# The first norm of a two-layer trunk: q and k of both token halves in four banks, the order of four engines given by hand

## The chip, the cores and the metric

The kernel runs on one core of one Trainium2 chip. The metric is device microseconds from start to end of the program. A core has TensorE (PE, with its weight load PEld), VectorE (DVE), ScalarE (ACT), GpSimd (POOL) and SyncE (SP), which here only issues DMAs. Products are written to eight PSUM banks of 128 x 512 float32.

## The reference

x and the result are 1024 tokens x 1024 features, float32. Two layers, each a token mixer and a SwiGLU, with adaLN: c gives shift, scale and gate of every sub-layer. The change touches only the beginning of layer 0:

```
mod = silu(c) @ ada_w[0] + ada_b[0]          # 6 x 1024: sh1, sc1, g1, sh2, sc2, g2
h = rms_norm(x, norm1_g[0]) * (1 + sc1) + sh1
q, k, v, f_logit = split(h @ w_in)           # 1024, 1024, 1024, 16 columns
cum = cumsum(log_sigmoid(f_logit + b_f))     # over the tokens
# 16 heads of 64: softmax(q k^T / 8 + cum_t - cum_s, causal) @ v, then w_out
```

Behind it come the attention's output product, the SwiGLU of layer 0, layer 1 (gated linear attention and a second SwiGLU) and a last norm.

## The kernel before, in words

**Precision.** Every large product is done in three float32r passes: operands are split into hi and lo (`split`, L159 cast on ACT, L160 subtract on DVE; weights by `load_w`, L202 on ACT, L205 three quarters on POOL and one on DVE), and `mm3` (L237 to L239) multiplies hi by hi, hi by lo, lo by hi.

**The first norm.** Eight tiles of 128 tokens (`xt`) are loaded; `ss_half` squares four of them on ACT with a sum (L439), takes rstd (DVE L441, a power on POOL L442) and scales the tiles by it. The work then runs over eight blocks d of 128 features. For each d, `ada0_mod` sums the rows of the adaLN matrix for shift and scale: 128 rows k times cact in eight pieces, of which NPE[d] go to PE as small matmuls (L462) and 8 - NPE[d] to DVE (L468 the first, L470 the others); two matmuls per column with ones (L472) add up the partitions into `mp`; DVE writes `modc` (L473) and `amul` (L333). `h_block(d, hf)` transposes four tiles of a token half to features by tokens (L479), scales and shifts on ACT (y, L481), rounds hi on ACT (L483) and subtracts lo on DVE or POOL (L484). `first_k` multiplies the block into three banks: f (16 gate columns, L491 and L492), q and k of the first head pair. `first_v` does the same for the values of the first half's tokens in two more banks (L817 to L819). All blocks of the first half are done, `first_evac` empties the banks (q: L603 to L607, k: L613 to L620, gates: L219, L220 and L780 to L786, after the second half the logarithm, the running sum `cum` over tokens and its way through DRAM to the tiles `cum_s`, which the attention's scores need); then the second half goes through the same banks.

**Behind it.** `v_half(0, 1)` makes the values of the second half (L237 to L239, output vps). Then for seven head pairs p `weave` interleaves `attention(p)` with the q, k and v products of the next pair (qk_b, vps_b), in proportion to planned costs. The sums for the other four adaLN parts of layer 0 (`ada_steps`, L367 and L369 on DVE) are spread over the same time.

**Order.** The program is written in one order, and a scheduler then sets the order of each engine's instructions by a timeline of its own; data dependencies are kept by semaphores, and an engine runs its instructions in the order that stands. Buffers are rings: a tile takes over a slot when the slot's last reader is done. SP issues DMAs in order. A few orders are pinned by hand further on (`issue_after`, the lags of `weave`).

Of the kernel before, what the change touches and what calls it, by code (L numbers as in the profile page):

```python
# [9 lines left out]
F32 = mybir.dt.float32  # L10
# [43 lines left out]
def trunk(ctx, tc, x, c, ada_w, ada_b, norm1_g, norm2_g, ffn_w_in, ffn_w_out,  # L54
# [244 lines left out]
    load_x(2)  # L299
    load_x(3)  # L300
    load_ada0(0)
    bf = cst.tile([16, 1], F32, name="bf")
    nc.sync.dma_start(bf, fox_b_f.rearrange("o h -> h o"))
# [32 lines left out]
    def ada_steps(l, j, acc_of, raw_of, w):  # L336
# [11 lines left out]
        for c0 in range(0, D, w):  # L348
            acc = acc_of([P, w], F32, f"acc{l}{j}{c0}")
            for k in range(8):  # L350
                if w == D or c0 == k == 0:
                    load()
                raw = got.popleft()
                if w < D:
                    load()
                    yield ADA_A
                    if k == 0:
                        nc.scalar.mul(acc, raw, cact[:, 0:1])
                    else:
                        nc.scalar.mul(raw, raw, cact[:, k:k + 1])  # L360
                        nc.gpsimd.tensor_add(acc, acc, raw)  # L361
                    yield ADA_B
                    continue
                for q in range(0, w, 256):
                    cs = slice(q, q + 256)
                    if k == 0:
                        nc.vector.tensor_scalar(acc[:, cs], raw[:, cs], cact[:, 0:1], None, op0=ALU.mult)  # L367
# [68 lines left out]
    def ss_half(hf):  # L436
        for t in range(4 * hf, 4 * hf + 4):
            sq = sqr([P, D], BF16, f"sq{t}")
            nc.scalar.activation(sq, xt[t], AF.Square, accum_out=ssx[:, t:t + 1])  # L439
        cs = slice(4 * hf, 4 * hf + 4)  # L440
        nc.vector.tensor_scalar(rstd[:, cs], ssx[:, cs], 1.0 / D, EPS, op0=ALU.mult, op1=ALU.add)  # L441
        nc.gpsimd.tensor_tensor(rstd[:, cs], rstd[:, cs], mhalf[:, 0:4], op=ALU.pow)  # L442
        for t in range(4 * hf, 4 * hf + 4):
            r = rstd[:, t:t + 1]
            if hf == 0 and t % 2 == 0:
                nc.vector.tensor_scalar(xt[t], xt[t], r, None, op0=ALU.mult)
            elif hf == 0 and t == 1:
                nc.scalar.activation(xt[t], xt[t], AF.Copy, scale=r)
            else:
                nc.gpsimd.tensor_scalar(xt[t], xt[t], r, 1.0, op0=ALU.mult, op1=ALU.mult)  # L450

    VLAG, XD = 1, 4
    NPE = (4, 4, 4, 0, 0, 0, 0, 0)

    def ada0_mod(d):

        npe = NPE[d]
        mp = mp0([P, 2], F32, f"mp{d}")
        part = lambda k: araw[(d, k // 4)][:, k % 4]
        for j in range(2):  # L460
            for k in range(npe):
                nc.tensor.matmul(mp[:, j:j + 1], part(k)[:, j, :], cact[:, k:k + 1], start=k == 0 and j == 0,  # L462
                                 stop=k == 7 and j == 1)
        if npe < 8:
            acc = sm.tile([P, 2, P], F32, tag="t1k", name=f"acc0{d}")
        for k in range(npe, 8):
            if k == npe:
                nc.vector.tensor_scalar(acc, part(k), cact[:, k:k + 1], None, op0=ALU.mult)  # L468
            else:
                nc.vector.scalar_tensor_tensor(acc, part(k), cact[:, k:k + 1], acc, op0=ALU.mult, op1=ALU.add)  # L470
        for j in range(2 if npe < 8 else 0):
            nc.tensor.matmul(mp[:, j:j + 1], acc[:, j, :], ones, start=npe == 0, stop=npe == 0 or j == 1)  # L472
        nc.vector.tensor_add(modc[:, 0, 0:2, d], mp, vec[:, d:d + 16:8])  # L473
        make_a(0, 0, slice(d, d + 1))

    def h_block(d, hf):
        tp = tp0([P, HALF], F32, f"xp{d}{hf}")
        for i in range(4):
            nc.tensor.transpose(tp[:, psl(i)], xt[4 * hf + i][:, psl(d)], ident)  # L479
        y = yv()  # L480
        nc.scalar.activation(y, tp, AF.Identity, scale=acol(0, 0, d), bias=mcol(0, 0, d))  # L481
        hi, lo = hT[d].hi[:, hsl(hf)], hT[d].lo[:, hsl(hf)]
        nc.scalar.copy(hi, y)  # L483
        (nc.gpsimd if d % 2 == 1 else nc.vector).tensor_sub(lo, y, hi.bitcast(F32))  # L484

    def first_acc(hf):
        return [(w, par([P, HALF], F32, f"{nm}s{hf}")) for nm, w in (("f", wf), ("q", wq0), ("k", wk0))]

    def first_k(d, hf, acc):
        ps = acc[0][1]  # L490
        nc.tensor.matmul(ps, wf[:, d, :], hT[d].hi[:, hsl(hf)], start=d == 0, stop=False)  # L491
        nc.tensor.matmul(ps, wf[:, d, :], hT[d].lo[:, hsl(hf)], start=False, stop=d == 7)  # L492
        for w, ps in acc[1:]:
# [282 lines left out]
    def first_evac(hf, acc):
        cs = hsl(hf)
        f = zt[:, cs]
        sum16(f, ze[:, cs], acc[0][1])
        nc.scalar.activation(ze[:, cs], f, AF.Abs, bias=bf)  # L780
        nc.vector.tensor_scalar(zt[:, cs], f, bf, 0.0, op0=ALU.add, op1=ALU.min)
        nc.scalar.activation(ze[:, cs], ze[:, cs], AF.Exp, scale=-1.0)
        if hf:
            nc.scalar.activation(ze, ze, AF.Ln, bias=1.0)
            nc.vector.tensor_sub(zt, zt, ze)
            nc.vector.tensor_tensor_scan(cum, zt, zt, 0.0, ALU.add, ALU.bypass)  # L786
            nc.sync.dma_start(cum_d, cum)
            load_cum(0)
            load_cum(1)
        q_evac(acc[1][1], qkt[0], hf)  # L790
        k_evac(acc[2][1], qkt[0], hf)
# [14 lines left out]
    vts[0] = []  # L806
    ss_half(0)
    acc = first_acc(0)
    vacc = [par([P, 2, 256], F32, f"vps0{tp}") for tp in range(2)]

    def first_v(d):
        wv = wvs[0][d // 4]
        for tp in range(2):
            for i in range(2):
                ts_ = psl(2 * tp + i)
                p_, a_ = vacc[tp][:, i, :], (hT[d].hi[:, ts_], hT[d].lo[:, ts_])
                nc.tensor.matmul(p_, a_[0], wv.hi[:, d % 4, :], start=d == 0 and i == 0, stop=False)  # L817
                nc.tensor.matmul(p_, a_[0], wv.lo[:, d % 4, :], start=False, stop=False)
                nc.tensor.matmul(p_, a_[1], wv.hi[:, d % 4, :], start=False, stop=d == 7 and i == 1)  # L819

    def pre(d):
        ada0_mod(d)
        if d + 3 < 8:
            load_ada0(d + 3)
        h_block(d, 0)

    pre(0)
    for d in range(8):
        if d == 0:
            feed.depth = 1  # L830
            wvs[0] = [feed.next()]
        if d == 2:
            wvs[0].append(feed.next())
        if d < 7:
            pre(d + 1)
        first_k(d, 0, acc)
        if d >= VLAG:
            first_v(d - VLAG)
        if d == XD:
            for t in range(4, 8):  # L840
                load_x(t)
            ss_half(1)
    for d in range(8 - VLAG, 8):
        first_v(d)
    first_evac(0, acc)
    acc = first_acc(1)
    for tp in range(2):
        v_split(0, tp, vacc[tp])
    h_block(0, 1)
    for d in range(8):  # L850
        if d < 7:
            h_block(d + 1, 1)
        first_k(d, 1, acc)
    first_evac(1, acc)
# [1034 lines left out]
```

## Time and profile before

| | |
|---|---|
| runs, median of 3 | 2449.29 us (2447.56 to 2454.5) |
| span of the profiled execution | 2446.2 us |
| its own time | not on the page; the median above stands beside it |
| PE busy | 2385.6 us, 98% of the span |
| DVE, ACT, POOL busy | 1701.0, 1193.2, 1151.3 us |
| q, k and f of the second half ready on PE | 97 us |
| first score evacuated with cum | 116.2 us |

Rows of a timeline read: start in us, busy us of the merged group, engine, line, operation, output <- inputs, shapes, count; in brackets the engine's idle time before it and what ended it. Rows of the stretches read: the stretch, its length, busy us and instructions of PE, PEld, DVE, ACT and POOL, the granted PE clock, the DMA share and GB/s. A PE row's length holds the draining of the pipeline, so the distance of two starts is the time that a product costs.

### The profile page before, as it was taken

The page shows a single profiled execution, that of the slowest core. Times are in us where ns is not written, and L with a number is a line of the kernel's source. Part 1 is how long each engine was busy: PE and PEld are TensorE (multiplying, and loading weights), DVE is VectorE, ACT ScalarE, POOL GpSimd, SP SyncE. Part 2 cuts the span into 40 slices and gives each one's busy share as a digit, 9 for nine tenths or more (in the row PEclk, how much of TensorE's full clock was granted, in tenths as well). Part 3 has the DMA queues.
Part 4 walks back from the last instruction along what each step waited for, and adds up shares of the span by engine and source line. Part 5 has one row for each costly group of instructions (what it writes and reads, how often), then busy time and mean ns, then how long its engine had stood idle before and what let it go on. Part 6 is the DMA issues. An engine that isn't in the chain of part 4 may idle for free.

```text
span 2446.2 us, 35525 instructions
## 1 busy us (share of the span) xinstructions
PE 2385.6 (98%) x12458; PEld 2030.6 (83%) x12458; DVE 1701.0 (70%) x2849; ACT 1193.2 (49%) x2281; POOL 1151.3 (47%) x1006
## 2 busy tenths in 40 slices
PE   6999999999999999999999999999999999999998
PEld 5888888888887878888888888888888888888878
DVE  7577777676686777665788455446487677665787
ACT  4665565675454443335324765564354333345325
POOL 4233333333347786653363544443336656653262
PEclk9999999999999999999999999999999999999999
DMA  8223333223425544347665333335325434347664
GB/s 269 79 87 121 103 96 113 70 95 113 137 98 195 184 164 162 124 162 263 227 214 174 94 100 102 100 104 173 100 80 191 147 134 155 130 168 257 233 206 148
DMA packets 318203, 359.19 MB, mean 147 GB/s; under 512 B 18044, under 2 KB 246552, under 8 KB 318024
## 3 DMA queue, kind: packets, MB, share of 16 engines
q1 hardware_dynamic: 318024, 356.92, 43.7%
q8 instruction: 98, 1.61, 0.3%
q14 instruction: 81, 0.66, 0.1%
HBM read 268.19 MB, written 88.67 MB: 146 GB/s over the span
## 4 chain that ended last, share of the span: by engine, by line
PE 81%; DVE 7%; ACT 3%; DMA 3%; POOL 2%; issue 2%; SPq 1%; DVEq 0%; POOLq 0%; ACTq 0%
PE p_b L237 15%; PE p_b L239 14%; PE p_b L238 14%; PE o_b L947 2%; PE t_b L933 2%; PE qk_b L237 2%; PE qk_b L238 2%; PE qk_b L239 2%; DMA ad_s<-in_ada_w_dram 2%; PE s_b L902 1%; PE s_b L903 1%; POOL ad_s L361 1%; DVE o_s L160 1%; PE vps_b L237 1%; PE vps_b L239 1%
## 5 line engine op out<-in xcount | busy, mean ns | idle before, releaser
L160 DVE TENSOR_TENSOR o_s<-xv_s,o_s 128x512 fp32r<-128x512 f32 (+1 forms) x376 | 326.4, 872 | 86.8 <-ACT o_s L159 86.0
L159 ACT CAST o_s<-xv_s 128x512 fp32r<-128x512 f32 (+1 forms) x376 | 217.4, 587 | 308.2 <-PE p_b L239 258.5
L237 PE MATMUL p_b<-B,o_s 128*128 128x512 f32 x608 | 237.2, 393 | 7.3 <-DVE x L1285 4.9
L238 PE MATMUL p_b<-B,o_s 128*128 128x512 f32 x608 | 238.5, 392 | 0.0
L239 PE MATMUL p_b<-B,o_s 128*128 128x512 f32 x608 | 238.0, 392 | 0.0
L913 POOL TENSOR_SCALAR lp_s<-lp_s,st 128x128 f32<-128x128 f32 (+7 forms) x128 | 95.9, 754 | 294.9 <-DVE st L912 266.2
L683 POOL TENSOR_TENSOR ex_s<-xv_s,xv_s 128x512 f32<-128x512 f32 (+1 forms) x64 | 90.2, 1409 | 250.6 <-DMA xv_s<-in_ffn_w_in_dram 88.9
L237 PE MATMUL p_b<-T,o_s 128*128 128x512 f32 x480 | 187.6, 391 | 0.0
L238 PE MATMUL p_b<-T,o_s 128*128 128x512 f32 x480 | 186.9, 389 | 0.0
L239 PE MATMUL p_b<-T,o_s 128*128 128x512 f32 x480 | 182.1, 390 | 0.0
L237 PEld LDWEIGHTS p_b<-B,o_s 128*128 128x128 f32 x608 | 115.0, 189 | 32.4 <-DVE x L1285 4.2
L239 PEld LDWEIGHTS p_b<-B,o_s 128*128 128x128 f32 x608 | 115.1, 189 | 24.0
L238 PEld LDWEIGHTS p_b<-B,o_s 128*128 128x128 f32 x608 | 115.1, 189 | 23.6
L911 ACT ACTIVATE lp_s<-lp_s,st 128x128 f32<-128x128 f32 (+7 forms) x128 | 99.3, 776 | 56.3 <-DVE st L907 55.7
L1285 DVE TENSOR_TENSOR ex_s<-ex_s,p_b 128x512 f32<-128x512 f32 x140 | 94.0, 681 | 34.2 <-PE p_b L239 34.0
L159 ACT CAST pt_s<-t_b 128x512 fp32r<-128x512 f32 (+1 forms) x160 | 80.1, 547 | 71.4 <-PE t_b L933 70.2
L685 POOL TENSOR_TENSOR xv_s<-ex_s,xv_s 128x512 f32<-128x512 f32 (+1 forms) x64 | 83.5, 1305 | 63.0 <-DVE o_s L160 61.1
L160 DVE TENSOR_TENSOR pt_s<-t_b,pt_s 128x512 fp32r<-128x512 f32 (+1 forms) x160 | 96.5, 630 | 17.9 <-ACT pt_s L159 17.3
L239 PEld LDWEIGHTS p_b<-T,o_s 128*128 128x128 f32 x480 | 90.3, 188 | 19.0
L237 PEld LDWEIGHTS p_b<-T,o_s 128*128 128x128 f32 x480 | 90.2, 188 | 18.5
L238 PEld LDWEIGHTS p_b<-T,o_s 128*128 128x128 f32 x480 | 90.2, 188 | 18.4
L907 DVE CUSTOM_DVE_ANT_0 lp_s<-s_b,cum_s 128x512 f32<-128x512 f32 (+3 forms) x128 | 72.6, 569 | 40.6 <-PE t_b L933 23.0
(1939 smaller groups left out, 7543.3 us busy)
## 6 DMA issues: line engine op xcount, KB each, us to landing
xv_s<-in_ffn_w_in_dram SPq DMA_DIRECT2D x176, 256.0 KB, 3.0
hid_B<-x SPq DMA_DIRECT2D x70, 512.0 KB, 2.6
ad_s<-in_ada_w_dram SPq DMA_DIRECT2D x96, 256.0 KB, 2.9
hid_T<-x SPq DMA_DIRECT2D x36, 512.0 KB, 2.7
xv_s<-in_ffn_w_out_dram SPq DMA_DIRECT2D x96, 192.0 KB, 3.9
ada_s<-in_ada_w_dram SPq DMA_DIRECT2D x32, 512.0 KB, 3.8
xv_s<-in_ffn_w_out_dram SPq DMA_DIRECT2D x40, 256.0 KB, 2.8
T2o<-hid_T SPq DMA_DIRECT2D x18, 512.0 KB, 8.0
```

Of the source, the lines that this page charges most:

```text
L159: nc.scalar.copy(hi, src)
L160: nc.vector.tensor_sub(lo, src, hi.bitcast(F32))
L237: nc.tensor.matmul(ps, ah, bh, start=start, stop=False)
L238: nc.tensor.matmul(ps, ah, bl, start=False, stop=False)
L239: nc.tensor.matmul(ps, al, bh, start=False, stop=stop)
L683: nc.gpsimd.tensor_add(s1, a21, a22)
L685: nc.gpsimd.tensor_sub(a11, s1, a11)
L907: nc.vector.tensor_tensor_reduce(lp[:, k0:k1], ps, cm[:, k0:k1], 1.0, mcur, ALU.add, ALU.min, mnew)
L911: nc.scalar.activation(lp, lp, AF.Exp, bias=mcur, scale=-1.0, accum_out=st[:, qi, 2:3])
L913: nc.gpsimd.tensor_scalar(lp, lp, st[:, qi, 3:4], 1.0, op0=ALU.mult, op1=ALU.mult)
L933: nc.tensor.transpose(tp[:, i, :], lps[qi][:, psl(2 * b + jj)], ident)
L1285: nc.vector.tensor_add(d, d if src is None else dest(G, src), ps)
```

## The change

q and k of both token halves get a bank each (four in all; the ring `par` goes from 5 to 4 banks, the transposes' ring from 2 to 3). The second half's blocks follow the first half's from d = 4 on, two per step (`LATE_H`), so that after step 7 both are through. The gate products (`first_f`, now after both halves, in two other banks) and the gates themselves (`gates`, both halves at once, 16 x 1024) come behind them, the values of the first half behind the gates, as `v_half(0, 0)`. The loads of the late tokens move ahead of the adaLN rows of d = 2 and 3; b_f and the gate weights, which stood ahead of wq and wk on SP, are loaded in steps 3 and 5. The whole block stands under `manual_schedule` for PE, DVE, ACT and POOL: those engines take their instructions from it in the written order (SP is left to the scheduler, and instructions of later parts may be put between). The first pieces of the other adaLN sums wait for the running sum of the gates (`held`). lo of the late half is always on POOL, that of the first half on DVE. NPE of d = 3 and 4 goes from 0 to 2.

```
-    par, tp0, mp0 = ps_rings(5, 2, 1)
+    par, tp0, mp0 = ps_rings(4, 3, 1)
...
-    bf = cst.tile([16, 1], F32, name="bf")
-    nc.sync.dma_start(bf, fox_b_f.rearrange("o h -> h o"))
-    wf = load_w16(W[:, 3 * D:3 * D + 16], "fw", wst)
-    wq0 = load_w(W[:, 0:P], "wq0", wst)
-    wk0 = load_w(W[:, D:D + P], "wk0", wst)
-    load_ada0(1)
-    load_ada0(2)
...
+                        with tc.issue_after(held[0]):
+                            nc.vector.tensor_scalar(acc[:, cs], raw[:, cs], cact[:, 0:1], None, op0=ALU.mult)
...
-    NPE = (4, 4, 4, 0, 0, 0, 0, 0)
+    NPE = (4, 4, 4, 2, 2, 0, 0, 0)
...
-        (nc.gpsimd if d % 2 == 1 else nc.vector).tensor_sub(lo, y, hi.bitcast(F32))
+        (nc.gpsimd if hf else nc.vector).tensor_sub(lo, y, hi.bitcast(F32))
...
+    def first_f(hf):
+        ps = psp.tile([P, HALF], F32, tag=f"b{4 + hf}", name=f"fs{hf}")
+        for d in range(8):
+            nc.tensor.matmul(ps, wf[:, d, :], hT[d].hi[:, hsl(hf)], start=d == 0, stop=False)
+            nc.tensor.matmul(ps, wf[:, d, :], hT[d].lo[:, hsl(hf)], start=False, stop=d == 7)
+        return ps
...
+    LATE_H = {4: (0, 1), 5: (2, 3), 6: (4, 5), 7: (6, 7)}
+    feed.depth = 1
+    with tc.manual_schedule(engines={ENG[e] for e in "PDAG"}):
+        ss_half(0)
+        for t in range(4):
+            scale_x(t)
+        mp = ada0_mp(0)
+        wq0 = load_w(W[:, 0:P], "wq0", wst)
+        wk0 = load_w(W[:, D:D + P], "wk0", wst)
+        load_ada0(1)
+        load_x(4)
+        load_x(5)
+        load_ada0(2)
+        load_x(6)
+        load_x(7)
+        load_ada0(3)
+        tp = x_trans(0, 0)
+        acc = ada0_acc(0)
+        ada0_out(0, mp, acc)
+        h_block(0, 0, tp)
+        acc0 = [[par([P, HALF], F32, f"{nm}s{hf}") for nm in "qk"] for hf in range(2)]
+        late = []
+        for d in range(8):
+            if d + 4 < 8:
+                load_ada0(d + 4)
+            if d < 7:
+                mp = ada0_mp(d + 1)
+                tp = x_trans(d + 1, 0)
+                acc = ada0_acc(d + 1)
+            first_qk(d, 0)
+            if d < 7:
+                ada0_out(d + 1, mp, acc)
+                h_block(d + 1, 0, tp)
+            if d == 2:
+                ss_half(1)
+            if d == 3:
+                for t in range(4, 8):
+                    scale_x(t)
+                bf = cst.tile([16, 1], F32, name="bf")
+                nc.sync.dma_start(bf, fox_b_f.rearrange("o h -> h o"))
+            if d == 5:
+                wf = load_w16(W[:, 3 * D:3 * D + 16], "fw", wst)
+                wvs[0] = [feed.next()]
+            if d == 7:
+                q_evac(acc0[0][0], qkt[0], 0)
+                k_evac(acc0[0][1], qkt[0], 0)
+            for e in LATE_H.get(d, ()):
+                h_block(e, 1, x_trans(e, 1))
+                late.append(e)
+                if len(late) > 1:
+                    first_qk(late[-2], 1)
+        first_qk(7, 1)
+        fs = [first_f(hf) for hf in range(2)]
+        wvs[0].append(feed.next())
+        q_evac(acc0[1][0], qkt[0], 1)
+        k_evac(acc0[1][1], qkt[0], 1)
+        gates(fs)
+        held = [next(i for i in reversed(nc.cur_bb.bb.instructions) if i.engine == ENG["D"])]
...
+    run(v_half(0, 0))
     run(v_half(0, 1))
```

`ada0_mp`, `ada0_acc` and `ada0_out` are `ada0_mod` cut in three (PE's own pieces; DVE's pieces; ones, modc and amul); `first_qk` is `first_k` without f; `x_trans` is the transposing part of `h_block`; `scale_x` is the scaling part of `ss_half`, with late tile 5 on ACT and the other late tiles on POOL; `gates` is the gate part of `first_evac` for 1024 tokens at once.

More of the change, by code (lines that the diff above doesn't have):

```diff
@@ L442, in ss_half, with scale_x, ada0_mp, ada0_acc @@
         nc.gpsimd.tensor_tensor(rstd[:, cs], rstd[:, cs], mhalf[:, 0:4], op=ALU.pow)
[L443 to L452, printed above, removed]
-    NPE = (4, 4, 4, 0, 0, 0, 0, 0)
-    def ada0_mod(d):
-        npe = NPE[d]
-        mp = mp0([P, 2], F32, f"mp{d}")
-        part = lambda k: araw[(d, k // 4)][:, k % 4]
[L460 to L467, printed above, removed]
+    def scale_x(t):
+        r = rstd[:, t:t + 1]
+        if t in (0, 2):
+            nc.vector.tensor_scalar(xt[t], xt[t], r, None, op0=ALU.mult)
+        elif t in (1, 5):
+            nc.scalar.activation(xt[t], xt[t], AF.Copy, scale=r)
+        else:
+            nc.gpsimd.tensor_scalar(xt[t], xt[t], r, 1.0, op0=ALU.mult, op1=ALU.mult)
+    NPE = (4, 4, 4, 2, 2, 0, 0, 0)
+    def ada0_mp(d):
+        mp = mp0([P, 2], F32, f"mp{d}")
+        for j in range(2):
+            for k in range(NPE[d]):
+                nc.tensor.matmul(mp[:, j:j + 1], araw[(d, k // 4)][:, k % 4, j, :], cact[:, k:k + 1],
+                                 start=k == 0 and j == 0, stop=False)
+        return mp
+    def ada0_acc(d):
+        part = lambda k: araw[(d, k // 4)][:, k % 4]
+        acc = sm.tile([P, 2, P], F32, tag="t1k", name=f"acc0{d}")
+        for k in range(NPE[d], 8):
+            if k == NPE[d]:
                 nc.vector.tensor_scalar(acc, part(k), cact[:, k:k + 1], None, op0=ALU.mult)
@@ L470, in ada0_mod, with ada0_out, x_trans @@
                 nc.vector.scalar_tensor_tensor(acc, part(k), cact[:, k:k + 1], acc, op0=ALU.mult, op1=ALU.add)
-        for j in range(2 if npe < 8 else 0):
-            nc.tensor.matmul(mp[:, j:j + 1], acc[:, j, :], ones, start=npe == 0, stop=npe == 0 or j == 1)
+        return acc
+    def ada0_out(d, mp, acc):
+        for j in range(2):
+            nc.tensor.matmul(mp[:, j:j + 1], acc[:, j, :], ones, start=NPE[d] == 0, stop=NPE[d] == 0 or j == 1)
         nc.vector.tensor_add(modc[:, 0, 0:2, d], mp, vec[:, d:d + 16:8])
         make_a(0, 0, slice(d, d + 1))
-    def h_block(d, hf):
+    def x_trans(d, hf):
         tp = tp0([P, HALF], F32, f"xp{d}{hf}")
@@ L483, in h_block, with first_qk @@
         nc.scalar.copy(hi, y)
[L484 to L493, printed above, removed]
-            mm3(ps, w.hi[:, d, :], w.lo[:, d, :], hT[d].hi[:, hsl(hf)], hT[d].lo[:, hsl(hf)], d == 0, d == 7)
+        (nc.gpsimd if hf else nc.vector).tensor_sub(lo, y, hi.bitcast(F32))
+    def first_qk(d, hf):
+        for w, ps in zip((wq0, wk0), acc0[hf]):
+            mm3(ps, w.hi[:, d, :], w.lo[:, d, :], hT[d].hi[:, hsl(hf)], hT[d].lo[:, hsl(hf)], d == 0, d == 7)
+    def first_f(hf):
[4 more added lines that the diff above has]
+        return ps
     def last_ins():
@@ L774, in trunk, with gates @@
     wvs = {}
[L776 to L791, printed above, removed]
+    def gates(fs):
+        for hf in range(2):
+            sum16(zt[:, hsl(hf)], ze[:, hsl(hf)], fs[hf])
+        nc.scalar.activation(ze, zt, AF.Abs, bias=bf)
+        nc.vector.tensor_scalar(zt, zt, bf, 0.0, op0=ALU.add, op1=ALU.min)
+        nc.scalar.activation(ze, ze, AF.Exp, scale=-1.0)
+        nc.scalar.activation(ze, ze, AF.Ln, bias=1.0)
+        nc.vector.tensor_sub(zt, zt, ze)
+        nc.vector.tensor_tensor_scan(cum, zt, zt, 0.0, ALU.add, ALU.bypass)
+        nc.sync.dma_start(cum_d, cum)
+        load_cum(0)
+        load_cum(1)
     def v_split(g, tp, ps):
@@ L804, in load_cum @@
         nc.sync.dma_start(cums[h], cum_d[h].partition_broadcast(P))
[L806 to L854, printed above, removed]
+    LATE_H = {4: (0, 1), 5: (2, 3), 6: (4, 5), 7: (6, 7)}
[56 more added lines that the diff above has]
+        held = [next(i for i in reversed(nc.cur_bb.bb.instructions) if i.engine == ENG["D"])]
```

3 lines of the change are left out of this document (2 added, 1 removed).

## Prediction

> **What bounds the kernel now.** I read the busy table by stretches first, since the change touches only the first norm.
>
> ```profile
> 0.00:60.00 60.00, 40.77 (x219) 35.86 (x219) 42.52 (x90) 27.81 (x45) 26.67 (x35) 0.95 0.87 274
> 60.00:116.00 56.00, 51.43 (x296) 45.22 (x297) 26.33 (x46) 32.87 (x54) 16.04 (x15) 0.93 0.25 74
> 116.00:560.00 444.00, 436.97 (x2865) 383.79 (x2864) 334.12 (x885) 273.25 (x591) 159.16 (x223) 1.00 0.32 100
> ```
>
> From 116 us on PE (first busy column) idles 7.0 us in 444, and the attention behind it is the same work. So PE is the bound there, and what the change is worth is how much later or earlier PE gets through the same products in the first 120 us. Two marks fix that. PE's timeline shows where the first norm's q, k and gate products (f) end and what follows:
>
> ```profile
> 96.79 0.39 PE L239 MATMUL ks_b<-h0h,wk0l_s 128*128 128x512 f32 x1
> 97.02 0.28 PE L237 MATMUL vps_b<-wv_4h_s,h0h 128*128 128x256 f32 x1
> 104.57 0.28 PE L239 MATMUL vps_b<-wv_4h_s,h0l 128*128 128x256 f32 x1
> 106.27 0.47 PE L237 MATMUL qk_b<-h0h,w_h_s 128*128 128x512 f32 x1 [0.81 <-DVE v_s L160]
> ```
>
> From 97.02 to 104.57 + 0.12 run 64 value products at 0.12 us; the values of all eight token tiles need 8 x 8 x 3 = 192, so 128 of them are already done at 97.0, in gaps of the first norm. The wait of 0.81 us is for a PSUM bank that a value tile gives back. Inside the first norm the engine that sets the pace is DVE, which sums the adaLN rows of one feature at a time:
>
> ```profile
> 62.89 0.99 PE L472 MATMUL mp_b<-ones,acc 128*128 128x1 f32 x4 [5.28 <-DVE acc L470]
> ```
>
> **The change, part by part.** The time depends on the new loop over features d, one chain: y and hi on ACT, lo on DVE, the next feature's sum on DVE (8 - NPE pieces, in this order behind lo), its matmuls with ones on PE, modc and amul on DVE, the next y. Its rows:
>
> ```profile
> 41.66 0.78 ACT L481 ACTIVATE y_s<-xp_b,modc,amul 128x512 f32<-128x512 f32 x1 [2.36 <-DVE amul L333]
> 42.47 0.62 ACT L483 CAST h0h<-y_s 128x512 fp32r<-128x512 f32 x1
> 49.57 0.68 DVE L484 TENSOR_TENSOR h0l<-y_s,h0h 128x512 fp32r<-128x512 f32 x1
> 45.51 0.34 DVE L468 TENSOR_SCALAR acc<-adas_s,cact 128x256 f32<-128x256 f32 x1
> 46.24 3.08 DVE L470 SCALAR_TENSOR_TENSOR acc<-adas_s,cact,acc 128x256 f32<-128x256 f32 x6
> 27.51 0.50 PE L472 MATMUL mp_b<-ones,acc 128*128 128x1 f32 x4
> 28.05 0.16 DVE L473 TENSOR_TENSOR modc<-mp_b,vec 128x2 f32<-128x2 f32 x1 [0.61 <-PE mp_b L472]
> ```
>
> y 0.80, hi 0.65, lo 0.69, ones 0.45, modc and amul to y 0.45: 3.0 us beside the sum. A sum of n pieces takes 0.35 + (n - 1) x 0.50 (3.08 / 6 = 0.51): 1.9, 2.9 and 3.9 us for n = 4, 6, 8. In the kernel before the scheduler let DVE sum the next features while ACT worked; the given order puts each sum behind the lo before it. Periods are then 4.9 (to d = 1 and 2), 5.9 (3 and 4) and 6.9 (5, 6, 7). The two pieces per column that NPE moves to PE for d = 3 and 4 are eight small matmuls in PE gaps, 0; without that cover some 0.1 us each.
>
> Three things lengthen periods. **(a)** To d = 4: the four squares of the late tokens stand on ACT behind hi of d = 3, and their rstd on DVE ahead of the sum of d = 4, so that sum waits for 4 x 1.2 less lo's 0.7, and rstd 0.2: +4.3.
>
> ```profile
> 44.66 1.06 ACT L439 ACTIVATE sq_s<-xt_s 128x1024 bf16<-128x1024 f32 x1 [1.57 <-DMA xt_s<-in_x_dram]
> 45.62 0.19 ACT L439 ACTIVATION_READ_ACCUMULATOR sq_s<-xt_s 128x1 f32 x1
> 51.79 1.26 POOL L442 TENSOR_TENSOR rstd<-rstd,mhalf 128x4 f32<-128x4 f32 x1 [7.07 <-DVE rstd L441]
> 54.62 4.99 POOL L450 TENSOR_SCALAR xt_s<-xt_s,rstd 128x1024 f32<-128x1024 f32 x4
> 58.55 3.20 DVE L367 TENSOR_SCALAR acc_s<-ada_s,cact 128x256 f32<-128x256 f32 x3
> 30.99 2.34 POOL L205 TENSOR_TENSOR wv_0l_s<-wv_s,wv_0h_s 128x256 fp32r<-128x256 f32 x3 [2.50 <-ACT wv_0h_s L202]
> 91.22 1.29 POOL L484 TENSOR_TENSOR h0l<-y_s,h0h 128x512 fp32r<-128x512 f32 x1 [2.41 <-ACT h0h L483]
> ```
>
> **(b)** Beside POOL a DVE piece that takes 0.35 alone takes 1.07 (3.20 / 3, at 58.55, while POOL scales x at 1.25 each): about one piece passes per POOL instruction. In the new order POOL's pow and three scalings (1.26 + 3 x 1.25 = 5.0) lie on the sum of d = 4: +3.0. Two lo of the late half (1.29 each) lie on d = 6: +2.2. Two lo and six weight quarters (2.6 + 6 x 0.78) lie on d = 7: its seven pieces go at POOL's 0.9, +3.4. **(c)** Splits of the weights for f, v and the next q stand on DVE among the pieces of d = 7: 0.3 + 0.5 + 0.5 = +1.3. Bounds for (b): 0, if no piece collides, to 10; I take 8.6.
>
> The start: the first sum now stands behind DVE's share of both weight splits.
>
> ```profile
> 8.32 3.38 SPq L303 DMA_DIRECT2D bf<-in_fox_b_f_dram  x1
> 19.19 1.14 ACT L202 CAST wk0h_s<-wk_s 128x512 fp32r<-128x512 f32 x2 [1.27 <-DMA wk_s<-in_fox_w_in_dram]
> 20.36 0.74 DVE L205 TENSOR_TENSOR wk0l_s<-wk_s,wk0h_s 128x256 fp32r<-128x256 f32 x1 [0.20 <-ACT wk0h_s L202]
> 20.25 0.78 ACT L481 ACTIVATE y_s<-xp_b,modc,amul 128x512 f32<-128x512 f32 x1
> 64.44 1.45 ACT L481 ACTIVATE y_s<-xp_b,modc,amul 128x512 f32<-128x512 f32 x2 [8.27 <-PE xp_b L479]
> ```
>
> With wk where it is, the sum runs 21.1 to 23.1 and y follows at 24.3, 4 us late; moving bf (3.38 us of SP) behind the ada loads can bring wk up to that much earlier, then y comes at 22.0. I take 23.3, +3.0 (bounds +1.8 and +4.0). Moved to d = 3, bf is covered: ada rows stand ready by then, and POOL, ACT and DVE set the pace.
>
> So y of d = 7 comes at 23.3 + 4.9 + 4.9 + 5.9 + 13.2 + 6.9 + 9.1 + 11.6 = **79.8**, against 65.1 now (second of the two at 64.44). Behind it: hi 81.2; y and hi of late features 4 and 5 on ACT 84.0, lo of 4 on POOL 83.9; the late products of 4 and the last early ones, 11 x 0.23, to 86.5; six ACT evacuations of the early banks, which stand ahead of the last two late y, to 90.1; those y and hi to 92.9; lo 94.2; the last q, k products 95.4; 32 gate products x 0.23 to **102.8**.
>
> ```profile
> 99.91 0.58 ACT L618 CAST KB<-ks_b 64x512 fp32r<-64x512 f32 x1
> 102.19 1.28 ACT L784 ACT_TABLE_LOAD   x1
> 103.49 1.06 ACT L784 ACTIVATE ze_s<-ze_s 16x1024 f32<-16x1024 f32 x1
> 104.58 1.22 DVE L785 TENSOR_TENSOR zt_s<-zt_s,ze_s 16x1024 f32<-16x1024 f32 x1 [1.70 <-ACT ze_s L784]
> 106.06 2.47 DVE L786 TENSOR_TENSOR_SCAN cum_s<-zt_s 16x1024 f32<-16x1024 f32 x1
> ```
>
> Then the lag of PE: f ends 102.8 - 97.0 = +5.8. As built, the order has only 26 value products ahead of that (the first half's values went behind the gates), so 128 - 26 = 102 x 0.12 = +12.2 more are left; they were free in gaps and now are not. The third value tile needs the first one's bank, whose split stands on ACT and DVE behind the gate chain: copy 0.58 (as at 99.91), add 0.7 (as lo), Abs 1.06 (as Ln), two table loads 2.56, Exp and Ln 2.1, subtract 1.22, half a split 0.4, scan 2.47, four held pieces 1.4, the other half 0.4 = 12.9 after f, against (96 - 26) x 0.12 = 8.4 of products to do: PE waits 4.5, for 0.81 now: +3.7. The attention's first score still comes under cover, since the values last as long as the chain to cum. Given back: PE's idle time behind 116 us, of which some 1.3 can fill.
>
> The clock: after PE's wait of 5.28 us products ran at half speed, then at full:
>
> ```profile
> 67.47 0.63 PE L238 MATMUL qs_b<-h0l,wq0h_s 128*128 128x512 f32 x1
> 69.18 0.40 PE L237 MATMUL qs_b<-h0h,wq0h_s 128*128 128x512 f32 x1
> ```
>
> (From 67.47 the next starts 0.43 later; the lengths 0.63 and 0.40 each hold some 0.2 of draining.) The new order leaves PE idle some 9 us ahead of d = 4, and half idle for 40 us. Bounds 0 (only waiting work is slowed) and +7.1 (below); I take +2.
>
> Sum: 5.8 + 12.2 + 3.7 - 1.3 + 2 = **+22.4 us** on the span of 2446.2: 2468.6. The page doesn't give this execution's own time; the median of the runs stands 3.1 us over the span, so 2471.7.
>
> **Rivals.** *PE at half clock throughout.* For: the row at 67.47, and products in bursts of 1.4 to 2.8 us; against: the stretch below, with gaps of PE of 1.0 us in ten and the granted clock (third number from the end) at 1.00.
>
> ```profile
> 40.00:50.00 10.00, 8.99 (x61) 7.73 (x59) 9.64 (x23) 6.10 (x11) 2.90 (x3) 1.00 1.08 381
> 51.67 0.48 DVE L470 SCALAR_TENSOR_TENSOR acc<-adas_s,cact,acc 128x256 f32<-128x256 f32 x1
> ```
>
> Price: ones of three features +0.5 each, 16 products on the path behind d = 7 x 0.20 = 3.2, and f's first 5 us at half speed (as now from 62.89 to past 67.47), 12 x 0.20 = 2.4: 7.1, in place of 2: 2476.8. The Trainium skill, "TensorE: Matmul & The Clock Gate", Part 1, has this rule: half rate after an idle window of about 3.4 us, full only after about 3.4 us of sustained work; by it no burst before f would restore the clock.
>
> *POOL does not collide* (the pieces fall between its instructions): 22.4 - 8.6 = +13.8, 2463.
>
> *The loose terms fall together* (no collision, no bank wait, wk early by 1.2, no clock term): 22.4 - 8.6 - 3.7 - 1.2 - 2 = +6.9, 2456, within 0.3%.
>
> *The second half really rides in the gaps* (faster). ada rows, not DVE, would pace it: the rows of d = 7 are in by about 51 (the row at 51.67 is one of its pieces now; DMA's share, 1.08 until 50, ends there), 8 pieces 3.9, ones to y 0.9: y at 55.8, then hi, lo, both halves' last products and f, 1.4 + 0.7 + 2.8 + 7.4, to 68.1. Lag 68.1 - 97.0 + 12.2 + 3.7 - 1.3 = -14.3: 2435. It decides from f ending before 82.4 (97.0 - 12.2 - 3.7 + 1.3). For: DMA near its limit early, POOL idle now; against: the given order on DVE and ACT, which leaves no freedom to sum ahead.
>
> **How the numbers follow.** Forecast as summed 0.47, half clock 0.17, no collision 0.16, loose terms 0.08, faster 0.12. Some 0.3% (7.3 us) is what a measurement here can tell: faster 0.12, same 0.08, slower 0.80. The range leaves out the last two cases and reaches from just above 2456 to the half clock with y(0) at its late bound and (b) at 10, 2476.8 + 2.4, and a scatter of 5 as the three runs show between 2447.56 and 2454.5, 2484.2: 2457 to 2485.
>
> **What would show it.** Right: y of feature 7 near 80, gaps of PE near 9 us ahead of the ones matmuls of feature 4, f ending near 103, PE idle 4 to 5 us ahead of the third value tile. Wrong: DVE pieces at 0.5 beside POOL, f ending before 85, or value products in the gaps ahead of f.

## The result, and the profile after

The changed kernel takes 2476.9 us (median of 4 runs, 2470.33 to 2479.37), the kernel before, run beside it, 2451.89 us (4 runs): the ratio is 1.0104, 95% interval 1.0085 to 1.0123. So it is slower by 1.0%, some 21 to 30 us. The profiled execution of after took 2476.98 us with a span of 2475.3, 29.1 more than the span of before.

Three stretches of after (columns as in the prediction: stretch, length, busy us and instructions of PE, PEld, DVE, ACT, POOL, granted clock, DMA share, GB/s):

```profile
0.00:60.00 60.00, 33.12 (x136) 26.82 (x137) 24.92 (x56) 23.29 (x35) 13.33 (x20) 0.85 0.80 248
60.00:120.00 60.00, 50.33 (x257) 41.66 (x255) 29.76 (x50) 32.52 (x50) 20.74 (x22) 0.83 0.12 36
145.00:580.00 435.00, 428.61 (x2813) 377.82 (x2812) 322.93 (x853) 266.73 (x574) 153.01 (x214) 1.00 0.31 96
```

In the first 60 us PE executes 136 instructions where it executed 219, and DVE is busy 24.92 us where it was 42.52. From 145 us on PE idles 6.4 us in 435, as before: the whole loss is in the front. How large it is can be read without the scatter of whole runs, from one instruction deep in the attention which both traces have, the evacuation of a later pair's k. Its row in before, and then in after:

```profile
277.64 0.68 DVE L619 TENSOR_TENSOR KLA<-qk_b,KA 64x512 fp32r<-64x512 f32 x1 [1.16 <-ACT KB L618]
```

```profile
306.08 0.68 DVE L623 TENSOR_TENSOR KLA<-qk_b,KA 64x512 fp32r<-64x512 f32 x1 [1.16 <-ACT KB L622]
```

It comes 28.4 us later. Below, this distance to 277.64 is called the **lag** of a kernel. From this mark to the end of the span all fourteen profiles of this study need 2166.0 to 2173.8 us, so what differs between them lies ahead of it, but for some 4 us either way.

The order of the front, from ACT's timeline of after: y of the features 0 to 7 (the rows that wait for amul or xp_b), and the copy of the second gate bank.

```profile
24.64 0.78 ACT L484 ACTIVATE y_s<-xp_b,modc,amul 128x512 f32<-128x512 f32 x1 [5.16 <-DVE amul L326]
32.63 0.78 ACT L484 ACTIVATE y_s<-xp_b,modc,amul 128x512 f32<-128x512 f32 x1 [6.56 <-DVE amul L326]
38.17 0.78 ACT L484 ACTIVATE y_s<-xp_b,modc,amul 128x512 f32<-128x512 f32 x1 [4.11 <-DVE amul L326]
44.33 0.78 ACT L484 ACTIVATE y_s<-xp_b,modc,amul 128x512 f32<-128x512 f32 x1 [4.74 <-DVE amul L326]
57.27 0.78 ACT L484 ACTIVATE y_s<-xp_b,modc,amul 128x512 f32<-128x512 f32 x1 [6.91 <-DVE amul L326]
64.94 0.78 ACT L484 ACTIVATE y_s<-xp_b,modc,amul 128x512 f32<-128x512 f32 x1 [5.20 <-DVE amul L326]
...
75.05 0.78 ACT L484 ACTIVATE y_s<-xp_b,modc,amul 128x512 f32<-128x512 f32 x1 [6.03 <-PE xp_b L479]
...
87.78 0.78 ACT L484 ACTIVATE y_s<-xp_b,modc,amul 128x512 f32<-128x512 f32 x1 [5.60 <-PE xp_b L479]
...
111.12 0.58 ACT L219 COPY ze_s<-fs 16x512 f32<-16x512 f32 x1 [3.05 <-PE fs L497]
```

y of feature 7 comes at 87.78 (forecast 79.8). PE's timeline of after shows the first period, the gap ahead of the ones matmuls of feature 4, the end of f and the wait for the third value tile's bank:

```profile
24.41 3.57 PE L454 MATMUL mp_b<-cact,adas_s 128*128 128x1 f32 x16 [0.26 <-DVE modc L473]
27.84 1.09 PE L479 MATMUL xp_b<-ident,xt_s 128*128 128x128 f32 x4
28.59 0.78 PE L237 MATMUL qs_b<-h0h,wq0h_s 128*128 128x512 f32 x1
29.16 0.63 PE L238 MATMUL qs_b<-h0l,wq0h_s 128*128 128x512 f32 x1
29.59 0.63 PE L239 MATMUL qs_b<-h0h,wq0l_s 128*128 128x512 f32 x1
...
31.30 0.85 PE L472 MATMUL mp_b<-ones,acc 128*128 128x1 f32 x4
...
55.76 1.01 PE L472 MATMUL mp_b<-ones,acc 128*128 128x1 f32 x4 [6.72 <-DVE acc L466]
...
110.69 0.39 PE L497 MATMUL fs<-h0l,fw_s 128*128 128x512 f32 x1
...
119.19 0.28 PE L239 MATMUL vps_b<-wv_4h_s,h0l 128*128 128x256 f32 x1
123.62 0.35 PE L237 MATMUL vps_b<-wv_0h_s,h0h 128*128 128x256 f32 x1 [4.15 <-DVE v_s L160]
```

PE goes through 24.41 to 32.15 without a gap, at half speed: the small matmuls take 3.57 us, and a product starts every 0.43 us. f ends at 110.9, 13.9 later than the 97.0 of before. The sums on DVE and what POOL does beside them, in after:

```profile
50.86 4.85 DVE L466 SCALAR_TENSOR_TENSOR acc<-adas_s,cact,acc 128x256 f32<-128x256 f32 x5
...
59.72 3.61 DVE L466 SCALAR_TENSOR_TENSOR acc<-adas_s,cact,acc 128x256 f32<-128x256 f32 x7
...
67.40 5.44 DVE L466 SCALAR_TENSOR_TENSOR acc<-adas_s,cact,acc 128x256 f32<-128x256 f32 x7
```

```profile
51.81 3.63 POOL L445 TENSOR_SCALAR xt_s<-xt_s,rstd 128x1024 f32<-128x1024 f32 x3
67.78 2.69 POOL L487 TENSOR_TENSOR h0l<-y_s,h0h 128x512 fp32r<-128x512 f32 x2 [12.34 <-ACT h0h L486]
```

Seven pieces take 3.61 us without POOL and 5.44 beside two lo of the late half.

### The profile page after: what moved, and what is told of

Its sections match the earlier page's. It is cut to its first block, busy times and chain, and to the rows that moved or that the text cites. A ratio compares the mean times of both kernels' runs of the same rounds, so it can differ in the third digit from the quotient of the medians.

```text
span 2475.3 us, 35555 instructions
## 1 busy us (share of the span) xinstructions
PE 2400.6 (97%) x12474; PEld 2040.0 (82%) x12474; DVE 1695.7 (69%) x2844; ACT 1195.4 (48%) x2280; POOL 1148.2 (46%) x1005
## 4 chain that ended last, share of the span: by engine, by line
PE 79%; DVE 8%; DMA 4%; ACT 4%; issue 3%; POOL 2%; SPq 0%; DVEq 0%; POOLq 0%; ACTq 0%
PE p_b L237 14%; PE p_b L239 14%; PE p_b L238 14%; PE o_b L957 2%; PE t_b L943 2%; PE qk_b L237 2%; PE qk_b L238 2%; PE qk_b L239 2%; DMA ad_s<-in_ada_w_dram 2%; PE s_b L912 1%; PE vps_b L237 1%; DVE o_s L160 1%; PE vps_b L239 1%; PE vps_b L238 1%; PE s_b L913 1%
## 5 line engine op out<-in xcount | busy, mean ns | idle before, releaser
L239 PEld LDWEIGHTS p_b<-B,o_s 128*128 128x128 f32 x608 | 115.5, 190 | 24.2
```

The source lines that it names most:

```text
L239: nc.tensor.matmul(ps, al, bh, start=False, stop=stop)
```

## The experiments

Theory A is that of the prediction: the chain y, hi, lo, sum, ones, modc, in the order given to the engines, sets the pace, with the squares and POOL on it, and value products that find no gap ahead of f come behind it. Its rival (B) is PE at half speed as the bound. A second rival, POOL's collisions, is priced in the runs on them. All measured in one table; y(7), f and lag are from one profiled execution of each kernel, the ratio from the times of all its runs; a dash stands where y(7) was not read.

| kernel | y(7), us | f ends, us | lag, us | lag less f's | ratio to before, 95% interval |
|---|---|---|---|---|---|
| after | 87.8 | 110.9 | +28.4 | 14.5 | 1.0104 (1.0085 to 1.0123) |
| e1 sum ahead | 84.0 | 107.2 | +24.3 | 14.1 | 1.0089 (1.0062 to 1.0117) |
| e2 squares early | 83.9 | 107.1 | +24.2 | 14.1 | 1.0091 (1.0072 to 1.0110) |
| e3 no late POOL | 84.9 | 106.9 | +24.0 | 14.1 | 1.0114 (1.0097 to 1.0131) |
| e4 PE kept busy | 100.2 | 124.6 | +43.5 | 15.9 | 1.0164 (1.0137 to 1.0190) |
| e5 ones first | 86.1 | 112.2 | +29.3 | 14.2 | 1.0112 (1.0084 to 1.0140) |
| e6 short chain | 80.0 | 102.9 | +19.1 | 13.3 | 1.0079 (1.0050 to 1.0108) |
| e7 ones first, values in loop | 90.6 | 120.3 | +32.6 | 9.4 | 1.0145 (1.0118 to 1.0172) |
| e8 no given order | 61.3 | 85.3 | +0.6 | 12.3 | 1.0027 (1.0014 to 1.0041) |
| e9 DVE's order free | 77.3 | 100.5 | +17.5 | 14.1 | 1.0073 (1.0054 to 1.0091) |
| e10 PE's order free | 87.8 | 107.7 | +22.7 | 12.0 | 1.0087 (1.0061 to 1.0114) |
| e11 no order, one value bank | – | 89.5 | -1.5 | 6.1 | 0.9991 (0.9981 to 1.0001) |
| e12 no order, two value banks | – | 92.3 | +2.4 | 7.1 | 1.0010 (0.9998 to 1.0021) |

"Lag less f's" is the lag less how much later than 97.02 f ended: what the value products and the bank wait behind f cost.

**e1, part of the sum (its first three pieces) ahead of lo.**

```
         nc.scalar.copy(hi, y)
+        if hf == 0 and d < 7:
+            ada0_acc(d + 1, 3)
         (nc.gpsimd if hf else nc.vector).tensor_sub(lo, y, hi.bitcast(F32))
```

> The first three pieces of each sum stand ahead of lo of the feature before it, where DVE idled 1.55 us a feature while ACT made y and hi. Theory A (the chain y, hi, lo, sum, ones in the given order sets the pace): the periods to d = 2 to 7 get 1.4 us shorter each, not that to d = 1, where PE ended the wait; y of feature 7 near 79.5 instead of 87.8, f ends near 102.5, time near 2468.5. Theory B (PE at half clock sets the pace): the ones still wait behind products at 0.43, so at most 3 us are won, y(7) near 85, time 2474.

y(7) gained 3.8 us where A said 8.3 and B at most 3. DVE's sums did end earlier, but then modc waited for PE (4.7, 2.7 and 2.2 us in the periods to d = 1, 2 and 3; the first of them):

```profile
32.25 0.16 DVE L478 TENSOR_TENSOR modc<-mp_b,vec 128x2 f32<-128x2 f32 x1 [4.65 <-PE mp_b L477]
```

Between the two theories: the chain is shorter, and PE is right behind it.

**e2, the squares early.** (`sq_x` makes one square; for the late half `ss_half` now holds rstd alone, which stands behind the sum of d = 4.)

```
+            if d == 3:
+                ss_half(1)
...
-            if d == 2:
-                ss_half(1)
+            for t in {1: (4, 5), 2: (6, 7)}.get(d, ()):
+                sq_x(t)
```

> The four late squares stand two by two behind hi of d = 2 and d = 3 on ACT, which idles 4 to 5 us there, and their rstd on DVE behind the sum of d = 4 instead of ahead of it. Theory A with collisions: the period to d = 4 falls from 12.9 to about 6.5, but POOL's scalings now lie on the sum of d = 5 and lengthen it by 2.3; y(7) near 83.7, time 2473. If POOL does not slow DVE: the period to 5 stays 7.7, y(7) near 81.4, time 2470.5. Theory B: the gap of 6.7 us of PE is gone, but PE stays at half speed as the bursts stay short.

The period to d = 4 fell from 12.9 to 6.6 and that to d = 5 grew from 7.7 to 8.9, y(7) came 3.8 earlier, 83.9 where A with collisions had 83.7. Part of that agreement is chance: the period to d = 2, which the edit does not touch, was 8.0 in this execution instead of 5.5, since PE did not reach full speed there; that took back 2.5, and y(0) happened to come 1.9 earlier.

**e3, no late work on POOL.** (The products of the late half read hi in place of lo, and three late tiles are not scaled.)

```
-        (nc.gpsimd if hf else nc.vector).tensor_sub(lo, y, hi.bitcast(F32))
+        if hf == 0:
+            nc.vector.tensor_sub(lo, y, hi.bitcast(F32))
...
-        else:
+        elif t < 4:
             nc.gpsimd.tensor_scalar(xt[t], xt[t], r, 1.0, op0=ALU.mult, op1=ALU.mult)
```

> Leaves out the scaling of late tiles 4, 6 and 7 and lo of the late half (its products read hi in place of lo, as many as before; lo is set to zero behind the gates). Theory A with collisions: the sum of d = 4 falls from 5.2 to 3.0 us, that of d = 6 from 5.8 to 4.0, that of d = 7 by 1 to 2 (the weight quarters on POOL stay), PE's waits for late lo go; y(7) near 82, f near 104, time near 2470. If the collisions are not the cause, the pieces stay as long as they are and the time at 2477.

The sums of d = 4 and 6 on DVE, in this kernel:

```profile
52.81 2.57 DVE L466 SCALAR_TENSOR_TENSOR acc<-adas_s,cact,acc 128x256 f32<-128x256 f32 x5
...
67.07 3.61 DVE L466 SCALAR_TENSOR_TENSOR acc<-adas_s,cact,acc 128x256 f32<-128x256 f32 x7
```

4.85 became 2.57 and 5.44 became 3.61, alike with the undisturbed 3.61: the collisions are shown, and they cost these sums 2.3 and 1.8 us. y(7) came at 84.9 where 82 was expected: the period to d = 6 fell by 0.5 only, since modc then waited 3.06 us for PE (1.77 in after), and the period to d = 2 took 7.6 where after has 5.5. f gained 4.0. The ratio is not lower than that of after; the lag of 24.0 lies at the lower end of its interval (0.97% of 2448 is 23.7), so only the front is read here.

**e4, dummy products (92 in all).**

```
             first_qk(d, 0)
+            for _ in range((8, 8, 8, 24, 12, 16, 16, 0)[d]):
+                nc.tensor.matmul(fill, wq0.hi[:, 0, :], hT[0].hi[:, hsl(0)], start=True, stop=True)
```

> Adds 100 dummy products 128x512 into a bank of their own (taken from the transposes) behind the q, k products of each step: 8, 8, 8, 24, 12, 16, 16. They keep PE busy ahead of the ones matmuls. Theory A: only what PE does on the chain gets faster: the period to d = 1 by 2.6, the ones by 0.3 in five features; y(7) near 83, time near 2472. Theory B (half clock is the main cost): all the 15 us of extra PE busy time go, f ends near 97, time near 2462. If the dummies themselves stand in the way (they run at 0.43), the periods get longer and the time passes 2480.

Neither A nor B: the third case came, 15.1 us more lag. The first batch ran at 0.37 a product (31.23 to 34.20), between the six q, k products and the ones:

```profile
30.80 0.63 PE L239 MATMUL ks_b<-h0h,wk0l_s 128*128 128x512 f32 x1
31.23 3.14 PE L838 MATMUL fill_b<-h0h,wq0h_s 128*128 128x512 f32 x8
34.20 0.50 PE L472 MATMUL mp_b<-ones,acc 128*128 128x1 f32 x4
```

What stands on PE ahead of the ones delays the chain where the sum is ready: the first eight took 3.0 us and the period to d = 1 grew by 2.6; the sixteen ahead of the ones of d = 7 took 3.6 and that period grew by 3.3. The 24 that fell into the wait for the sum of d = 4 cost nothing (12.8 us against 12.9). The run does not tell what a full speed for free would have been worth.

**e5, ones ahead of the products.**

```
                 acc = ada0_acc(d + 1)
+                ada0_out(d + 1, mp, acc)
             first_qk(d, 0)
...
-                ada0_out(d + 1, mp, acc)
```

> The ones matmuls of the next feature stand on PE ahead of the q, k products of this one instead of behind them, nothing else. Theory A (the chain y, hi, lo, sum, ones, modc; PE at 0.43 a product stands on it where the ones wait behind six products): the period to d = 1 falls from 8.0 to about 5.5 (PE's small matmuls and transposes still take 4.5), that to d = 7 by 0.7, the others by nothing, since the sum ended them; y(7) near 84.3, f ends near 107.5, time near 2473.5. Theory B (PE is the bound throughout): the products only move behind the ones, y(7) and f stay within 1 us, time 2477.

The period to d = 1 fell to 5.5, as A said; but the next one grew from 5.5 to 7.6. PE's timeline says why:

```profile
27.54 0.95 PE L472 MATMUL mp_b<-ones,acc 128*128 128x1 f32 x4
28.36 0.77 PE L237 MATMUL qs_b<-h0h,wq0h_s 128*128 128x512 f32 x1
...
31.06 3.41 PE L454 MATMUL mp_b<-cact,adas_s 128*128 128x1 f32 x16
34.33 1.09 PE L479 MATMUL xp_b<-ident,xt_s 128*128 128x128 f32 x4
35.22 0.85 PE L472 MATMUL mp_b<-ones,acc 128*128 128x1 f32 x4
```

From one ones to the next PE has no gap: 2.7 of products, 3.3 of small matmuls, 0.9 of transposes, 0.8 of ones, 7.7 in all at half speed. Where four pieces of a sum are on PE, PE at half speed is the bound, and its order did not matter: the two periods make 13.1 us, 13.5 in after. B holds for these features. The lag is 0.9 higher for a reason further on: y(7) came 1.6 earlier, but from y(7) to the end of f it took 26.0 us where after took 23.1, since the six products of d = 6 now stand behind the ones of d = 7 and the late y wait for their transposes (1.75 and 1.17 us).

**e6, a short chain.** e1, e2 and e5 together, four pieces of every sum on PE, the evacuation of the first banks behind the last late y.

```
-    NPE = (4, 4, 4, 2, 2, 0, 0, 0)
+    NPE = (4, 4, 4, 4, 4, 4, 4, 4)
```

> Ones ahead of the products; three pieces of the next sum ahead of lo; four pieces of every sum on PE (NPE 4 throughout), so that DVE has four; late squares two by two behind hi of d = 2 and 3; the evacuation of the first half's banks behind the last late y. Theory A: the chain is 0.8 + 0.65 + 0.7 + 0.5 + 0.85 + 0.45 = 4.0 a feature, y(7) near 58, f ends near 78, the attention lags by 78 - 97 + 14.5 = -5, time near 2444. Theory B: PE needs 1.8 + 0.7 + 1.0 + 2.6 = 6.1 us a feature at half speed and 3.3 more for a late one: y(7) near 72, f near 94, time near 2460.

y(7) came at 80.0, later than both theories had it. B had the cause right but the price too low: 1.8 for a feature's small matmuls that take 3.3 (from 37.72 to 40.99); in the late steps PE waited another 2.3 us for lo from POOL. A row of its stretches, and of its PE timeline:

```profile
23.00:45.00 22.00, 22.00 (x88) 20.36 (x89) 9.11 (x24) 7.78 (x13) 0.00 (x0) 1.00 1.08 334
```

```profile
37.72 3.41 PE L458 MATMUL mp_b<-cact,adas_s 128*128 128x1 f32 x16
40.99 1.09 PE L488 MATMUL xp_b<-ident,xt_s 128*128 128x128 f32 x4
...
45.29 1.96 PE L458 MATMUL mp_b<-cact,adas_s 128*128 128x1 f32 x16
```

PE is busy 22.00 of 22.00 us, and at half speed until 45 us; then the same x16 take 1.96.

**e7, e5 with the first 256 tokens' values inside the loop.**

```
-    par, tp0, mp0 = ps_rings(4, 3, 1)
+    par, tp0, mp0, va0 = ps_rings(4, 2, 1, 1)
...
+    LATE_V = {4: (0, 1), 5: (2, 3), 6: (4, 5), 7: (6, 7)}
...
+            if d in (3, 5):
+                wvs.setdefault(0, []).append(feed.next())
...
+            for e in LATE_V.get(d, ()):
+                first_v(e)
```

> As the one with the ones first, and the values of the first 256 tokens go into a bank of their own inside the loop, 12 products a step from d = 4 on (48 in all), their weights loaded in steps 3 and 5. Theory A (value products behind f cost 0.12 each because the gaps ahead of f stay empty): the attention's lag falls by 48 x 0.12 = 5.8 less what of the 26 that fill the gap ahead of f today is lost, and less 1 to 2 by which they hold up the loop: 2 to 4 below the kernel with ones first alone. Rival: at 0.21 each on PE, and two more weight quarters on POOL and DVE, they hold up the loop by as much as they save: within 1 us of it.

Worse than the rival: what is left behind f fell by 4.8 us (14.2 to 9.4), near the 5.8 expected, but f came 8.1 later. In a given order, work put into the gaps holds up the chain, and not only by the products. The period to d = 5 grew by 3.7 against e5 (7.7 to 11.4) before the first value product ran (68.88). There the splits of the weights, now loaded in step 3, stand on DVE ahead of the sum and ahead of modc, and the second one waits for its load. Rows of ACT and DVE:

```profile
65.38 1.14 ACT L202 CAST w_h_s<-w__s 128x512 fp32r<-128x512 f32 x2 [5.48 <-DMA w__s<-in_fox_w_in_dram]
66.55 0.54 DVE L205 TENSOR_TENSOR w_l_s<-w__s,w_h_s 128x256 fp32r<-128x256 f32 x1 [1.36 <-ACT w_h_s L202]
67.01 0.15 DVE L473 TENSOR_TENSOR modc<-mp_b,vec 128x2 f32<-128x2 f32 x1
```

Another 3.7 came between y(7) and the end of f (29.7 us, 26.0 in e5); there a late y waited 3.73 us for its transposes, behind twelve value products at 0.21.

**e8, the same kernel without the given order.**

```
-    with tc.manual_schedule(engines={ENG[e] for e in "PDAG"}):
+    with ExitStack():
```

> The changed kernel without the given order: the scheduler places the block's instructions on all engines, everything else (banks, gates behind both halves, held sums, loads) as changed. Theory A (the given order keeps DVE from summing ahead): DVE sums while ACT works, y(7) falls back to about 70 (65 in the kernel before), f near 95, and the 14.5 us between f's lag and the attention's shrink only by what fills gaps: time near 2462. If the banks and the changed order of loads are the cause, the time stays at 2477.

This settles the main question. Its mark and its first stretch:

```profile
278.23 0.68 DVE L623 TENSOR_TENSOR KLA<-qk_b,KA 64x512 fp32r<-64x512 f32 x1 [1.16 <-ACT KB L622]
```

```profile
0.00:60.00 60.00, 41.08 (x186) 34.81 (x186) 42.38 (x87) 32.60 (x52) 28.38 (x35) 0.89 0.91 277
```

DVE is busy 42.38 us in the first 60 again (24.92 in after), y(7) comes at 61.3, f ends 11.7 earlier than in before, and with the same banks, loads, gates and held sums the lag is 0.6 instead of 28.4. So 27.8 of it belong to the given order, in these two executions. The 12.3 us behind f stay, and eat what f gained. (By the times the given order costs less, 1.0104 less 1.0027, some 19 us: this kernel's times stand 0.27% over before, 6.6 us, of which the front explains 0.6. What makes the rest is open. The profiled execution was the fastest of its ten.)

**e9 and e10, one engine's order set free** (e9, DVE's, is shown; e10, PE's, has `"DAG"`).

```
-    with tc.manual_schedule(engines={ENG[e] for e in "PDAG"}):
+    with tc.manual_schedule(engines={ENG[e] for e in "PAG"}):
```

> The changed kernel with the order given for PE, ACT and POOL only; DVE's is the scheduler's. If DVE's given order is what costs (each sum behind lo and behind rstd of the late tokens), this comes near the kernel without any given order: the attention lags by 1 to 8 us instead of 28, time 2450 to 2457. If it is the combination (squares on ACT ahead of the late y, products on PE ahead of the ones), sums made ahead still wait on PE and ACT: the lag stays over 15, time 2463 or more.

> The changed kernel with the order given for DVE, ACT and POOL only; PE's is the scheduler's. With DVE's order free the attention's lag fell from 28.4 to 17.5 us, with all four free to 0.6. If PE's order is the other part (ones behind products, value products not in the gaps), the lag falls here by some 10 to 17 us, time 2460 to 2466. If PE only follows what DVE, ACT and POOL give it, and the parts count only together, the lag stays over 24, time near 2473.

DVE's freedom is worth 10.9 us of lag, PE's 5.8, both alone, all four together 27.8: the second case for e9, and for e10 neither of its numbers. (In e10's execution the period to d = 2 took 8.0 us, in that of after 5.5, so its 5.8 may be 2.5 too small.) In e9 the sums are ready ahead, and in the first features PE, at half speed, becomes the bound:

```profile
20.00:36.00 16.00, 15.49 (x63) 14.16 (x63) 9.58 (x24) 2.79 (x4) 1.56 (x3) 1.00 1.10 355
```

In e10 PE still waits for the sums, whose order is given. Its waits between 18 and 140 us (total, times, longest; 13.8 us in all in after, the longest 6.7):

```profile
PE mp_b L472 <- DVE acc L466: 10.1, 4, 4.1
```

**e11 and e12, no given order and values in banks of their own inside the loop** (e7's edit, weights loaded in steps 2 and 4; e12 with two banks and one for the transposes, `ps_rings(4, 1, 1, 2)`).

```
-    par, tp0, mp0 = ps_rings(4, 3, 1)
+    par, tp0, mp0, va0 = ps_rings(4, 2, 1, 1)
```

> No given order, and the values of the first 256 tokens in a bank of their own inside the loop (48 products, their weights loaded in steps 2 and 4, the transposes' ring one bank shorter). Without the given order PE still waits some 8 us between 18 and 60 us and 1.9 us for a value bank. If the empty gaps are what is left of the cost, the attention leads the kernel before by 3 to 5 us, time 0.1 to 0.2% below it. If PE's work at half speed fills them (products in bursts at 0.21 instead of 0.12), it stays at +1, time equal to the one without given order.

> No given order, the values of all first-half tokens inside the loop (96 products, two banks; the transposes keep one bank). By the gaps: as the kernel with one value bank or 1 to 3 us faster still, and no wait for a value bank. If the one bank for transposes holds up the loop (a transpose waits for the y of the block before it), y of feature 7 comes later than 61 us and what is won is lost: 2450 to 2456.

With one bank the part behind f halves (12.3 to 6.1), f comes 4.1 later, and the kernel leads before by 1.5 us at the mark: 2446.4 against 2447.87 us, a ratio of 0.9991 that may be 1; that is less than the 3 to 5 us of the first case. With two banks f comes another 2.9 later and nothing is won: ACT waits 12.4 us for transposes up to 92 us, 4.1 with one bank, which is the second case. No kernel here is shown to be faster than the one before.

## Why the prediction was right, and where not

The forecast was +22.4 us; the lag is 28.4, the span 29.1, and the medians of the times stand 25.0 apart. Sign and cause hold; one term was too small.

- **From y(7) to the end of f** the forecast had 23.0 us; it is 110.9 - 87.8 = 23.1.
- **Behind f** the forecast had 12.2 + 3.7 - 1.3 = 14.6; it is 14.5. The wait for the third tile's bank is 4.15 (4.5 forecast), and e7 and e11 show that value products placed ahead of f do shorten this part.
- **y(7)** was forecast for 79.8 and came at 87.8. This is the step that failed: "Periods are then 4.9 (to d = 1 and 2)" left out what PE itself has to do in them, at the speed that it has there. The periods were 8.0, 5.5, 6.2, 12.9, 7.7, 10.1 and 12.7, against 4.9, 4.9, 5.9, 13.2, 6.9, 9.1 and 11.6; y(0) came 1.3 later than taken, 0.3 past its bound: the first sum, beside POOL's split of wk, took 3.05 us instead of 1.9 (its last three pieces 2.21), and its ones 1.0 instead of 0.45. Of the 8.0 us, 3.1 are the period to d = 1, where six products and eight small matmuls (x16: the trace has two records for each) at half speed fill PE; e5 shows that the order of PE does not cure it. The eight small matmuls of d = 3 and 4 were priced at 0.1 each; at half speed the four of d = 3 take 1.72 us (37.94 to 39.66), 0.43 each. The last three periods are 0.8 to 1.1 longer since modc waits 1.2 to 1.8 us for the ones, where 0.45 was taken. Rows of DVE and POOL in after, the first two for y(0):

```profile
19.78 2.50 POOL L205 TENSOR_TENSOR wk0l_s<-wk_s,wk0h_s 128x256 fp32r<-128x256 f32 x3
20.87 2.21 DVE L466 SCALAR_TENSOR_TENSOR acc<-adas_s,cact,acc 128x256 f32<-128x256 f32 x3
...
64.49 0.16 DVE L473 TENSOR_TENSOR modc<-mp_b,vec 128x2 f32<-128x2 f32 x1 [1.17 <-PE mp_b L472]
...
74.60 0.16 DVE L473 TENSOR_TENSOR modc<-mp_b,vec 128x2 f32<-128x2 f32 x1 [1.77 <-PE mp_b L472]
...
87.33 0.16 DVE L473 TENSOR_TENSOR modc<-mp_b,vec 128x2 f32<-128x2 f32 x1 [1.27 <-PE mp_b L472]
```

The period to d = 1 could have been read in the profile of before: there too y(1) comes 8.5 us behind y(0) (20.25 to 28.79), with eight small matmuls (x16) at half speed between them:

```profile
20.06 3.55 PE L462 MATMUL mp_b<-cact,adas_s 128*128 128x1 f32 x16 [0.30 <-DVE modc L473]
...
28.79 0.78 ACT L481 ACTIVATE y_s<-xp_b,modc,amul 128x512 f32<-128x512 f32 x1 [7.11 <-DVE amul L333]
```

- **The clock** was a term of its own, +2, set beside the chain. It belongs in the chain. The rival "half clock throughout" named 2476.8, which is what came, but by luck: f ran at 0.23 a product from its first one (32 from 103.67 to 110.9), and the products behind d = 7 were at full speed, while the periods of the first features, which it did not count, paid. The granted clock of 1.00 that was set against it decides nothing (last section). The +2 is luck too: it made up for a quarter of the 8.0 us that y(7) came late.
- **The squares (a)** were right: PE idled 6.7 us ahead of the ones of feature 4 (near 9 forecast), and e2 takes 6.3 off that period.
- **POOL (b)** was right in kind and near in size. 8.6 was taken; the three sums are longer by 2.3, 1.8 and 3.6, together 7.7, than undisturbed ones. That POOL's work holds up DVE there is shown by e3 for the first two; the third is not tested. The Trainium skill, "SBUF — State Buffer", section "Who interferes with whom", has a rule by which a DVE instruction with two SBUF inputs contends with a GpSimd instruction that reads SBUF; the 4.85 against 2.57 us agrees.
- **"POOL does not collide", "the loose terms fall together" and "the second half rides in the gaps"** did not come. The argument against the last one, that the given order leaves no freedom to sum ahead, is what e8 shows: with the freedom f ends at 85.3. That is still later than the 82.4 from which the prediction let the change win.
- **bf moved behind**: nothing waited for it, as priced.

What stays open: how the 27.8 us of the given order divide. The engines' parts do not add up (10.9 and 5.8 of 27.8), since each freed engine meets the next one's fixed order.

## What to carry to other kernels

An order written out by hand fixes on every engine which wait comes next: before giving it, list for each engine what would stand ready behind the waiting instruction, since that is what the scheduler used here (DVE busy 42.4 us of the first 60 against 24.9). Price a step by the busiest engine in it at the speed which it has there, small matmuls included, and not only by the chain that looks longest. And when products are moved out of a stretch with gaps to behind it, they cost their time there even where the stretch itself gets shorter (e8: f 11.7 earlier, 12.3 behind it).

## What the runs showed of the hardware

PE ran at half speed with no gap at all: in e6 the profile has it busy 22.00 us of 22.00 (the row at 23.00) with products 0.43 us apart; it reaches full speed at 45.3 us and is back at half by 49. The granted clock in that row reads 1.00: the column does not show this state, only the distance of two starts does. (In before, between 40 and 50 us, it reads 1.00 as well, and there products start 0.23 apart.) The Trainium skill, "TensorE: Matmul & The Clock Gate", Part 1, has full rate after some 3.4 us of sustained work; these 22 us do not agree with it. Over half of that time (3.3 + 0.7 of each 7.6) is matmuls of one column. In e4 full speed, reached in the course of the first eight dummies (the ones at 34.20 take 0.50), is lost again at 37.2, with one-column matmuls and transposes between and no gap over 0.26 us. That such work does not count as activity would fit both, but no run here separates it. Whether PE caught full speed for a moment differed between executions with the same order up to there: the period to d = 2 took 5.5 us in after, 8.0 in e2 and 7.6 in e3, and with it the front scatters by 2.5 us.
